# Dense products of a two-layer hybrid decoder step: the 576 tokens as 256 and 320 columns instead of 288 and 288

## The chip, the core and the metric

The kernel runs on one core of one Trainium2 chip. The metric is device time in microseconds for one execution. Column n of a product is token n: the 512 prompt tokens come first, then 8 samples of 8 tokens, 576 in all.

## What is computed

Two decoder layers for a prompt of 512 tokens and 8 samples of 8 tokens each, with shared weights. Cut to what matters here:

```python
h = rmsnorm(x, ln_mix)
parts = split(h @ w_in)                 # 1024 -> 8712 columns: three branches and three gates
o_a = hgrn2(...); o_b = diff_attention(...); o_c = gated_deltanet(...)
mix = sum(sigmoid(gate_i) * (o_i @ w_branch_i))     # 512 -> 1024 each
x = x + mix @ w_out                                 # 1024 -> 1024
g, u = split(rmsnorm(x, ln_ffn) @ w_up)             # 1024 -> 2 * 2816
g = causal_dwconv(g, width 3)
x = x + (silu(g) * u) @ w_down                      # 2816 -> 1024
```

The q, k and v of the gated DeltaNet go through a causal convolution of width 4. All of it is float32, with new states and key and value rows as further outputs.

## The kernel before, in words

Activations lie transposed: features on the 128 partitions, the 576 tokens along the free axis. A dense product takes one 128-column tile of a weight matrix at a time. `dense_steps` (L266) loads it from memory, `split` (L262) makes of it a rounded part `wh` (ScalarE) and the rest `wl` (VectorE), both float32r, four 128x128 blocks at a time; activations are split the same way into `xh` and `xl`. Per block of 128 input features, TensorE then does `xh wh`, `xl wh` and `xh wl`, each in two matmuls because a sum of 576 columns does not fit one PSUM bank: tokens 0 to 287 (`hf` = 0) into one bank and 288 to 575 (`hf` = 1) into another. So a block is six matmuls, each with a weight load of its own, in the order `xh wh`, `xl wh` (first tokens), `xh wh`, `xl wh` (second), `xh wl` (first), `xh wl` (second). The accumulator `acc` is a tile of two banks, of which two alternate (`psA`).

One block's six matmuls go through the helper `mm` (L181, the matmul itself on L189), which also adds `n / 2400` us to a planner's clock `clk`. In the mixing part of a layer `drive` (L317) uses that clock to interleave the products with the recurrences, the attention and their own small float32 matmuls; the order of instructions on every engine is fixed when the program is built. The steps of the run, by the profile's time: start (0 to 20 us), mixing part of layer 0 (20 to 668), the merge of the branches (L1414 on, 668 to 819, with the output projection up to 819 to 825), the convolution MLP (825 to 1233: 22 gate tiles, 22 up tiles, then the down projection in three groups), then the same again for layer 1 to 2449.6.

A finished sum is read out of PSUM by VectorE or ScalarE. Most readers take both halves in one instruction through a view `v2` that cuts the other operand in two; the two convolution inputs need three, since prompt and samples go to different places: `conv_silu` (L721, 24 times, tile `cb`) and the MLP gate (L1476, 44 times, tile `cbf`):

```python
tt(P[:, 2:2 + HALF], acc[:, 0], rb[:, 0:HALF], ALU.mult)                 # 288 columns
tt(P[:, 2 + HALF:514], acc[:, 1, 0:224], rb[:, HALF:SEQ], ALU.mult)      # 224 columns
tt(Ps[:, :, 2:10], acc[:, 1, 224:288]..., rb[:, SEQ:]..., ALU.mult)      # 64 columns
```

Of the kernel before, what the change touches and what calls it, by code (L numbers as in the profile page):

```python
# [10 lines left out]
F32 = mybir.dt.float32  # L11
# [5 lines left out]
ALU = mybir.AluOpType  # L17
# [5 lines left out]
SEQ = 512  # L23
# [4 lines left out]
T = SEQ + NS  # L28
HALF = T // 2
# [117 lines left out]
def kernel(ctx, tc, a, o, depth=DEPTH, dbg=None):  # L147
    nc = tc.nc
    V, S, G, PE = nc.vector, nc.scalar, nc.gpsimd, nc.tensor
# [9 lines left out]
    psA = pool('psA', bufs=2, space=PSUM)  # L159
# [21 lines left out]
    def mm(out, lhsT, rhs, start=True, stop=True, cost=None, **kw):  # L181
        n = math.prod(rhs.shape[1:])
        if lhsT.dtype == F32R:
            clk[0] += n / 2400
        elif lhsT.dtype == BF16:
            clk[0] += 0.107
        else:
            clk[0] += cost or (0.094 if kw else max(n / 600, 0.214))
        PE.matmul(out, lhsT, rhs, start=start, stop=stop, **kw)  # L189
# [5 lines left out]
    def tt(out, in0, in1, op, eng=None):  # L195
        (eng or V).tensor_tensor(out=out, in0=in0, in1=in1, op=op)  # L196
# [27 lines left out]
    for k in range(KD):  # L224
        x_ = px.tile([128, T], F32, name=f'x{k}')
# [40 lines left out]
    def dense_steps(src, xs, M=128, raws=None, nk=None, prime=False):  # L266

        nk, k = nk or len(xs), 0  # L270
        gr = [(k0, min(4, nk - k0)) for k0 in range(0, nk, 4)]
        if raws is None:
            raws = []
            for k0, n in gr:
                raw = wp.tile([128, 512], F32, tag='raw', bufs=4, name='raw')
                nc.sync.dma_start(raw[:, :n * M], src[:, k0 * M:(k0 + n) * M])
                raws.append(raw)

        def weights(g):
            n = gr[g][1] * M  # L280
            wh = wp.tile([128, 512], F32R, tag='wh', bufs=3, name='wh')
            wl = wp.tile([128, 512], F32R, tag='wl', bufs=3, name='wl')
            split(raws[g][:, :n], wh[:, :n], wl[:, :n])
            return wh, wl

        nxt = weights(0)
        if prime:
            yield
        acc = psA.tile([128, 2, 512], F32, tag='acc', name='acc')
        for g, (k0, n) in enumerate(gr):  # L290
            wh, wl = nxt
            for i in range(n):
                if i == min(1, n - 1) and g + 1 < len(gr):
                    nxt = weights(g + 1)
                xh, xl = xs[k]
                cs = slice(i * M, (i + 1) * M)
                for w, xx in ((wh, (xh, xl)), (wl, (xh,))):
                    for hf in range(2):
                        for x_ in xx:
                            mm(acc[:M, hf, :HALF], w[:, cs], x_[:, hf * HALF:(hf + 1) * HALF],  # L300
                               start=(k == 0 and w is wh and x_ is xh), stop=(k == nk - 1 and w is wl))
                k += 1
                if k < nk:
                    yield
        return acc[:, :, :HALF]

    def dense(src, xs):
        return run(dense_steps(src, xs))
# [8 lines left out]
    def drive(stages, fill, xs, pre, psmp):  # L317
# [53 lines left out]
        while True:  # L371
# [41 lines left out]
                assert not live and not stages  # L413
                return
            clk[0] = min(ts)

    def v2(ap):
        return ap.rearrange('p (a b) -> p a b', a=2)

    def norm_in(k, xt, g):  # L420

# [169 lines left out]
    with stage('ln0', 'right') as p0:  # L591
# [12 lines left out]
        rb, rc = norms()  # L604
# [33 lines left out]
    for l in range(depth):  # L638
# [62 lines left out]

        def half(dst, acc):

            V.scalar_tensor_tensor(out=v2(dst), in0=acc, scalar=0.5, in1=v2(rb), op0=ALU.mult, op1=ALU.mult)

        def gate_post(i, acc):
            th = gt.tile([128, T], F32, tag='th', name='thb')
# [13 lines left out]
        def conv_silu(acc, ci, dst):  # L721

            P = cvp.tile([128, 604], F32, tag='cb', name='cb')
            Ps = P[:, 515:603].rearrange('p (b j) -> p b j', j=11)
            G.memset(P[:, 0:3], 0.0)
            G.tensor_copy(Ps[:, :, 0:3], hg[:, ci])
            tt(P[:, 3:3 + HALF], acc[:, 0], rb[:, 0:HALF], ALU.mult)
            tt(P[:, 3 + HALF:515], acc[:, 1, 0:224], rb[:, HALF:SEQ], ALU.mult)
            tt(Ps[:, :, 3:11], acc[:, 1, 224:288].rearrange('p (b j) -> p b j', j=8),
               rb[:, SEQ:].rearrange('p (b j) -> p b j', j=8), ALU.mult)  # L730
            G.tensor_copy(gco[:, ci, 0, :], P[:, 512:515])
            G.tensor_copy(gco[:, ci, 1:9, :], Ps[:, :, 8:11])
            A = cvp.tile([128, 604], F32, tag='ca', name='ca')
            w = F['gconv']
            S.activation(A[:, 0:600], P[:, 0:600], AF.Copy, scale=w[:, 4 * ci:4 * ci + 1])
            for j in range(1, 4):
                V.scalar_tensor_tensor(out=A[:, 0:600], in0=P[:, j:j + 600], scalar=w[:, 4 * ci + j:4 * ci + j + 1],  # L737
                                       in1=A[:, 0:600], op0=ALU.mult, op1=ALU.add)
            th = gt.tile([128, 604], F32, tag='th', name='ct')
            S.activation(th[:, 0:600], A[:, 0:600], AF.Tanh, scale=0.5)  # L740
            sv = lambda t: t[:, 515:603].rearrange('p (b j) -> p b j', j=11)[:, :, 0:8]
            V.scalar_tensor_tensor(out=dst[:, 0:SEQ], in0=th[:, 0:SEQ], scalar=1.0, in1=A[:, 0:SEQ], op0=ALU.add, op1=ALU.mult)
            V.scalar_tensor_tensor(out=dst[:, SEQ:].rearrange('p (b j) -> p b j', j=8), in0=sv(th), scalar=1.0, in1=sv(A),
                                   op0=ALU.add, op1=ALU.mult)
# [246 lines left out]
        def hgrn_head(h, p):  # L991
            f2 = lambda tag, bufs=1: p.tile([128, T], F32, tag=tag, bufs=bufs, name=tag)
            acc = yield win(16 + 4 * h + 0)
            XX, xn = p.tile([128, 2, TP], F32, name='XX'), [0]
# [4 lines left out]
                return XX[:, xn[0] % 2]  # L999

            E = XX[:, 0, 0:T]
            tt(v2(E), acc, v2(rb), ALU.mult)
            S.activation(E, E, AF.Exp, scale=-1.0)
            V.tensor_scalar(out=E, in0=E, scalar1=float(2.0 ** 60), scalar2=None, op0=ALU.min)
            lf, f_, k_, Gc = f2('lf'), f2('f'), f2('k'), f2('G')
# [6 lines left out]
            acc = yield win(16 + 4 * h + 1)  # L1012
            th = gt.tile([128, T], F32, tag='th', name='th')
# [3 lines left out]
            V.scalar_tensor_tensor(out=q_, in0=th, scalar=1.0, in1=hx, op0=ALU.add, op1=ALU.mult)  # L1017
            acc = yield win(16 + 4 * h + 2)
            hv = flip()
            S.copy(v2(hv[:, 0:T]), acc)  # L1020
            vt = p.tile([128, 5, 128], F32, name='vt')
            yield 0.8
            transpose_to(vt, hv, rc)
# [73 lines left out]
            for cc in range(4):  # L1097
                cs = slice(128 * cc, 128 * cc + 128)
# [8 lines left out]
                if cc:  # L1107
                    V.scalar_tensor_tensor(out=Sn, in0=Sc, scalar=eG[:, 128 * cc + 127:128 * cc + 128], in1=pu[:, 0:128],
                                           op0=ALU.mult, op1=ALU.add)
# [30 lines left out]
        def qk_prep(ti, gi, p):  # L1140
            acc = yield win(ti)
            xr = p.tile([128, TP], F32, tag='xr', bufs=2, name='xr')
            G.memset(xr[:, T:], 0.0)
            S.copy(v2(xr[:, 0:T]), acc)
            tm = p.tile([128, 5, 128], F32, tag='tm', bufs=2, name='tm')
            yield 0.9
            transpose_to(tm, xr)
# [33 lines left out]
        def diff_head(h, p):  # L1181
# [3 lines left out]
            acc = yield win(32 + 3 * h + 2)  # L1185
            xr = p.tile([128, TP], F32, tag='xr', bufs=2, name='xr')
            G.memset(xr[:, T:], 0.0)
            S.copy(v2(xr[:, 0:T]), acc)
            vt = p.tile([128, 5, 128], F32, name='vt')
            yield 0.9  # L1190
            transpose_to(vt, xr, rc)
# [218 lines left out]
        p = pmix  # L1410
# [3 lines left out]
        for f in range(KD):  # L1414
            m = p.tile([128, T], F32, tag='m', bufs=2, name='m')
            for i in range(3):
                th = gt.tile([128, T], F32, tag='th', name='th')
                nc.sync.dma_start(th, thd[l][8 * i + f])
                acc = dense(a['w_br'][l, i, f], brs[4 * i:4 * i + 4])
                if i == 0:  # L1420
                    V.scalar_tensor_tensor(out=v2(m), in0=v2(th), scalar=1.0, in1=acc, op0=ALU.add, op1=ALU.mult)
                else:
                    t = p.tile([128, T], F32, tag='ol', bufs=2, name='mt')
                    V.scalar_tensor_tensor(out=v2(t), in0=v2(th), scalar=1.0, in1=acc, op0=ALU.add, op1=ALU.mult)
                    tt(m, m, t, ALU.add)
            xh = pm.tile([128, T], F32R, name=f'mh{f}')
            xl = pm.tile([128, T], F32R, name=f'ml{f}')
            split(m, xh, xl)
            mixs.append((xh, xl))
# [8 lines left out]
        def residual(f, acc, src, dst, keep):  # L1438
            xo = p.tile([128, T], F32, tag='xo', bufs=2, name='xo')
            nc.sync.dma_start(xo, src[f])  # L1440
            xn = keep.tile([128, T], F32, tag=f'x{f}', name=f'x{f}') if keep is not None else p.tile([128, T], F32, tag='xn', bufs=2, name='xn')
            V.scalar_tensor_tensor(out=v2(xn), in0=acc, scalar=0.5, in1=v2(xo), op0=ALU.mult, op1=ALU.add)  # L1442
            nc.sync.dma_start(dst[f], xn)
            return xn

# [16 lines left out]
        for gidx, ng in enumerate(FG):  # L1462
            hid = []
            for i in range(ng):
# [3 lines left out]
                if fi == 0:  # L1468
# [4 lines left out]
                Ps = P[:, 514:594].rearrange('p (b j) -> p b j', j=10)  # L1473
                G.memset(P[:, 0:2], 0.0)
                G.tensor_copy(Ps[:, :, 0:2], hf_[:, fi])
                tt(P[:, 2:2 + HALF], acc[:, 0], rb[:, 0:HALF], ALU.mult)  # L1476
                tt(P[:, 2 + HALF:514], acc[:, 1, 0:224], rb[:, HALF:SEQ], ALU.mult)
                tt(Ps[:, :, 2:10], acc[:, 1, 224:288].rearrange('p (b j) -> p b j', j=8),
                   rb[:, SEQ:].rearrange('p (b j) -> p b j', j=8), ALU.mult)
                G.tensor_copy(fco[:, fi, 0, :], P[:, 512:514])  # L1480
                G.tensor_copy(fco[:, fi, 1:9, :], Ps[:, :, 8:10])
# [12 lines left out]
                                       op0=ALU.add, op1=ALU.mult)  # L1494
                tt(s2, s2, rb, ALU.mult)
                acc = run(g)
                tt(v2(s2), v2(s2), acc, ALU.mult)
                hh = ph.tile([128, T], F32R, tag='hh', bufs=9, name='hh')
                hl = ph.tile([128, T], F32R, tag='hl', bufs=9, name='hl')
                split(s2, hh, hl)  # L1500
# [144 lines left out]
```

## Time and profile before

| | |
|---|---|
| median of 3 runs | 2452.12 us (2451.75 to 2452.2) |
| the profiled execution | 2451.43 us, of which the span from first to last instruction is 2449.6 us |
| TensorE matmuls, weight loads | 2420.2 us busy (99%), 2317.4 us (95%), 19602 each |
| VectorE, ScalarE, GpSimd | 1664.6 us (68%), 1119.8 us (46%), 131.9 us (5%) |
| granted TensorE clock, mean | 0.997 |

PE is the stream of matmuls, PEld that of weight loads, DVE is VectorE, ACT ScalarE, POOL GpSimd, SP the engine that issues most DMAs. A matmul's own duration in the profile holds its way through the array and overlaps its neighbours; what one costs in a stream is the distance from one start to the next, called its pitch below.

### The profile page before, as it was taken

What the parts mean: (1) busy time and instruction counts of PE and PEld (TensorE: products, weight loads), DVE (VectorE), ACT (ScalarE), POOL (GpSimd) and SP (SyncE); (2) the same over time, 40 slices, a digit from 0 to 9 for tenths busy, and PEclk for the clock granted to TensorE, in tenths of its full rate; (3) what the DMA queues carried; (4) which work ended last, traced back from release to release, by engine and by line L of the source; (5) the groups of instructions that cost most, each with busy time, mean ns of one, the idle gap of its engine ahead of it and who ended that gap; (6) DMA issues with size and microseconds to landing.
All of it is one profiled execution on the core that took longest, in us unless ns stands there. A gap on an engine that the chain in (4) does not pass through costs nothing.

```text
span 2449.6 us, 51852 instructions
## 1 busy us (share of the span) xinstructions
PE 2420.2 (99%) x19602; PEld 2317.4 (95%) x19602; DVE 1664.6 (68%) x4156; ACT 1119.8 (46%) x2401; POOL 131.9 (5%) x446
## 2 busy tenths in 40 slices
PE   8999999999999999999999999999999999999999
PEld 7999989899999999999999998988989999999999
DVE  7787787778665663646677877868776556646464
ACT  5556555646433332323455665646554233323232
POOL 1000000100000010101000010100000000001010
PEclk9999999999999999999999999999999999999999
DMA  6234564554465325252442245564635553242524
GB/s 211 94 99 133 163 215 148 181 179 147 132 204 180 118 87 164 83 162 86 145 137 93 92 163 167 181 211 138 220 103 156 181 175 109 91 155 85 165 84 127
DMA packets 222841, 352.90 MB, mean 144 GB/s; under 512 B 36864, under 2 KB 71680, under 8 KB 222592
## 3 DMA queue, kind: packets, MB, share of 16 engines
q1 hardware_dynamic: 221008, 346.78, 44.1%
q8 instruction: 155, 2.54, 0.4%
q10 hardware_dynamic: 1584, 2.82, 0.4%
q14 instruction: 94, 0.77, 0.1%
HBM read 288.90 MB, written 60.60 MB: 143 GB/s over the span
## 4 chain that ended last, share of the span: by engine, by line
PE 89%; DVE 6%; ACT 3%; issue 1%; DMA 1%; SPq 0%; ACTq 0%; DVEq 0%
PE acc L189 72%; PE r L189 13%; PE r L193 3%; DVE dtr L196 1%; DVE wl L196 1%; DMA ctt<-dt 0%; DVE XX L196 0%; DVE s L527 0%; DVE ca L737 0%; ACT wh L263 0%; DMA x<-in_xT 0%; ACT P L1235 0%; ACT ks L773 0%; DMA og<-ogd 0%; DVE ot L196 0%
## 5 line engine op out<-in xcount | busy, mean ns | idle before, releaser
L189 PE MATMUL acc<-xh,wh 128*128 128x288 f32 x3584 | 1019.3, 299 | 4.1 <-ACT wh L263 4.1
L189 PE MATMUL acc<-xl,wh 128*128 128x288 f32 x3584 | 1012.2, 297 | 1.1 <-DVE xl L425 0.9
L189 PE MATMUL acc<-xh,wl 128*128 128x288 f32 x3584 | 767.0, 294 | 5.0 <-DVE wl L196 4.7
L263 ACT CAST wh<-raw 128x512 fp32r<-128x512 f32 x624 | 383.2, 615 | 835.4 <-PE acc L189 787.5
L189 PEld LDWEIGHTS acc<-xh,wh 128*128 128x128 f32 x3584 | 675.1, 188 | 20.1 <-issue 12.7
L189 PEld LDWEIGHTS acc<-xl,wh 128*128 128x128 f32 x3584 | 675.9, 189 | 3.6 <-DVE xl L425 1.8
L189 PEld LDWEIGHTS acc<-xh,wl 128*128 128x128 f32 x3584 | 577.4, 188 | 7.8 <-DVE wl L196 6.8
L196 DVE TENSOR_TENSOR wl<-raw,wh 128x512 fp32r<-128x512 f32 x624 | 423.0, 679 | 178.5 <-ACT wh L263 177.4
L189 PE MATMUL acc<-hl,wh 128*128 128x288 f32 x704 | 196.7, 296 | 0.0
L189 PE MATMUL acc<-hh,wh 128*128 128x288 f32 x704 | 194.3, 292 | 0.0
L189 PE MATMUL acc<-hh,wl 128*128 128x288 f32 x704 | 147.2, 290 | 0.0
L189 PEld LDWEIGHTS acc<-hl,wh 128*128 128x128 f32 x704 | 132.3, 188 | 0.0
L189 PEld LDWEIGHTS acc<-hh,wh 128*128 128x128 f32 x704 | 132.0, 188 | 0.0
L189 PEld LDWEIGHTS acc<-hh,wl 128*128 128x128 f32 x704 | 113.2, 188 | 0.0
L189 PE MATMUL acc<-oL,wh 128*128 128x288 f32 x384 | 108.0, 295 | 0.0
L189 PE MATMUL acc<-oh,wh 128*128 128x288 f32 x384 | 107.3, 295 | 0.0
L196 DVE TENSOR_TENSOR cbf<-acc,rb 128x288 f32<-128x288 f32 x132 | 39.0, 351 | 88.9 <-PE acc L189 85.0
L1486 DVE SCALAR_TENSOR_TENSOR caf<-cbf,fm,caf 128x592 f32<-128x592 f32 x88 | 73.5, 835 | 15.9 <-ACT caf L1484 14.3
L189 PE MATMUL acc<-oh,wl 128*128 128x288 f32 x384 | 81.6, 293 | 0.0
L1442 DVE SCALAR_TENSOR_TENSOR xn<-acc,xo 128x576 f32<-128x576 f32 x40 | 30.3, 758 | 70.8 <-PE acc L189 70.8
L189 PEld LDWEIGHTS acc<-oL,wh 128*128 128x128 f32 x384 | 73.0, 190 | 0.0
L189 PEld LDWEIGHTS acc<-oh,wh 128*128 128x128 f32 x384 | 72.1, 188 | 0.0
(427 smaller groups left out, 3631.1 us busy)
## 6 DMA issues: line engine op xcount, KB each, us to landing
raw<-in_w_in_t SPq DMA_DIRECT2D x272, 256.0 KB
raw<-in_w_up SPq DMA_DIRECT2D x176, 256.0 KB
pg<-in_kT SPq DMA_DIRECT2D x128, 256.0 KB
pg<-in_v SPq DMA_DIRECT2D x128, 256.0 KB
raw<-in_w_dn SPq DMA_DIRECT2D x64, 256.0 KB
xo<-xres SPq DMA_DIRECT2D x56, 288.0 KB
thd<-thb SPq DMA_DIRECT2D x48, 288.0 KB
th<-thd SPq DMA_DIRECT2D x48, 288.0 KB
```

Source lines behind the costliest of these rows:

```text
L189: PE.matmul(out, lhsT, rhs, start=start, stop=stop, **kw)
L193: PE.transpose(out, in_, idm)
L196: (eng or V).tensor_tensor(out=out, in0=in0, in1=in1, op=op)
L263: S.copy(hi, src)
L1442: V.scalar_tensor_tensor(out=v2(xn), in0=acc, scalar=0.5, in1=v2(xo), op0=ALU.mult, op1=ALU.add)
L1486: V.scalar_tensor_tensor(out=A[:, 0:592], in0=P[:, j:j + 592], scalar=w[:, 3 * fi + j:3 * fi + j + 1], in1=A[:, 0:592], op0=ALU.mult, op1= ...
```

## The change

The two halves become 256 and 320 columns. The accumulator is one tile of 1024 columns over two banks; the first 256 tokens go to columns 256 to 511 (the end of the first bank), the other 320 to columns 512 to 831 (the start of the second). So the sums of all 576 tokens lie side by side, and every reader takes a plain 128x576 operand. The three instructions of each convolution input become two, of 512 and 64 columns. Number and order of the matmuls, weight loads and DMAs stay, and `mm` still books (256 + 320) / 2400 us for each pair.

```diff
-        acc = psA.tile([128, 2, 512], F32, tag='acc', name='acc')
+        acc = psA.tile([128, 1024], F32, tag='acc', name='acc')
...
                 for w, xx in ((wh, (xh, xl)), (wl, (xh,))):
-                    for hf in range(2):
+                    for t0, t1 in ((0, 256), (256, T)):
                         for x_ in xx:
-                            mm(acc[:M, hf, :HALF], w[:, cs], x_[:, hf * HALF:(hf + 1) * HALF],
+                            mm(acc[:M, 256 + t0:256 + t1], w[:, cs], x_[:, t0:t1],
                                start=(k == 0 and w is wh and x_ is xh), stop=(k == nk - 1 and w is wl))
...
-        return acc[:, :, :HALF]
+        return acc[:, 256:256 + T]
...
-            V.scalar_tensor_tensor(out=v2(dst), in0=acc, scalar=0.5, in1=v2(rb), op0=ALU.mult, op1=ALU.mult)
+            V.scalar_tensor_tensor(out=dst, in0=acc, scalar=0.5, in1=rb, op0=ALU.mult, op1=ALU.mult)
...
-                tt(P[:, 2:2 + HALF], acc[:, 0], rb[:, 0:HALF], ALU.mult)
-                tt(P[:, 2 + HALF:514], acc[:, 1, 0:224], rb[:, HALF:SEQ], ALU.mult)
-                tt(Ps[:, :, 2:10], acc[:, 1, 224:288].rearrange('p (b j) -> p b j', j=8),
+                tt(P[:, 2:514], acc[:, 0:SEQ], rb[:, 0:SEQ], ALU.mult)
+                tt(Ps[:, :, 2:10], acc[:, SEQ:].rearrange('p (b j) -> p b j', j=8),
                    rb[:, SEQ:].rearrange('p (b j) -> p b j', j=8), ALU.mult)
```

`conv_silu` changes like the last hunk, and the other readers of a sum (the gates, the residual adds, the copies before a transpose, the merge, the product with the up part) like the one above it: `v2(...)` goes, the operands stay.

## Rows read from the trace of the kernel before

**Rows 1.** The page, busy time of each engine: us, share of the span, instructions.
```profile
PE 2420.2 (99%) x19602; PEld 2317.4 (95%) x19602; DVE 1664.6 (68%) x4156; ACT 1119.8 (46%) x2401; POOL 131.9 (5%) x446
```

**Rows 2.** Who PE waited for, the two longest: us in total, times, longest.
```profile
PE acc L189 <- DVE wl L196: 4.7, 6, 2.0
PE acc L189 <- ACT wh L263: 4.1, 2, 2.0
```

**Rows 3.** Groups by line and shape, one matmul of each kind of activation: xcount | busy, mean ns.
```profile
L189 PE MATMUL acc<-xh,wh 128*128 128x288 f32 x3584 | 1019.3, 299 | 4.1 <-ACT wh L263 4.1
L189 PE MATMUL acc<-hh,wh 128*128 128x288 f32 x704 | 194.3, 292 | 0.0
L189 PE MATMUL acc<-oh,wh 128*128 128x288 f32 x384 | 107.3, 295 | 0.0
L189 PE MATMUL acc<-mh,wh 128*128 128x288 f32 x256 | 71.1, 292 | 0.0
```

**Rows 4.** The chain of waits in order of time, unbroken runs of dense matmuls: start, us, count.
```profile
128.64 6.25 PE acc L189 x48
135.44 6.33 PE acc L189 x48
210.52 13.70 PE acc L189 x102
...
666.66 151.64 PE acc L189 x1149
825.18 407.22 PE acc L189 x3132
1877.10 157.60 PE acc L189 x1197
2041.58 404.11 PE acc L189 x3108
```

**Rows 5.** Timeline of PE in the MLP of layer 0: start, us, one matmul.
```profile
900.22 0.29 PE L189 MATMUL acc<-xh,wh 128*128 128x288 f32 x1
900.35 0.30 PE L189 MATMUL acc<-xl,wh 128*128 128x288 f32 x1
```

**Rows 6.** Stretch of layer 0 (columns as in rows 12; clock 0.50), and PE's timeline there.
```profile
398.00:399.50 1.50, 1.50 (x7) 1.50 (x7) 0.76 (x2) 0.00 (x0) 0.00 (x0) 0.50 1.00 361
...
398.81 0.44 PE L189 MATMUL acc<-xl,wh 128*128 128x288 f32 x1
399.05 0.44 PE L189 MATMUL acc<-xh,wh 128*128 128x288 f32 x1
399.29 0.41 PE L189 MATMUL acc<-xl,wh 128*128 128x288 f32 x1
```

**Rows 7.** Timeline, plain float32 matmuls of 256 columns, from two starts, merged: us, count.
```profile
250.42 1.24 PE L189 MATMUL r<-ckq 128*128 128x256 f32 x5
...
250.64 0.81 PE L189 MATMUL r<-ckq 128*128 128x256 f32 x3
```

**Rows 8.** Timeline of PEld in a stream of 64-column float32 matmuls: loads of 128x128.
```profile
611.81 0.97 PEld L189 LDWEIGHTS r<-XX 128*128 128x128 f32 x8
```

**Rows 9.** Timeline, a dense matmul whose successor's weight load comes late: PE, then PEld.
```profile
440.73 0.29 PE L189 MATMUL acc<-xh,wh 128*128 128x288 f32 x1
440.86 0.29 PE L189 MATMUL acc<-xl,wh 128*128 128x288 f32 x1
441.73 0.53 PE L189 MATMUL acc<-xh,wl 128*128 128x288 f32 x2 [0.57 <-DVE wl L196]
...
440.73 0.19 PEld L189 LDWEIGHTS acc<-xl,wh 128*128 128x128 f32 x1
441.73 0.30 PEld L189 LDWEIGHTS acc<-xh,wl 128*128 128x128 f32 x2 [0.80 <-DVE wl L196]
```

**Rows 10.** Timeline of one MLP gate tile's read-out: last matmuls of the sum, then DVE.
```profile
910.75 0.29 PE L189 MATMUL acc<-xh,wl 128*128 128x288 f32 x1
911.14 0.89 DVE L196 TENSOR_TENSOR cbf<-acc,rb 128x288 f32<-128x288 f32 x3 [2.06 <-PE acc L189]
```

**Rows 11.** Groups by line and shape, readers of a sum on DVE.
```profile
L196 DVE TENSOR_TENSOR s<-s,acc 128x576 f32<-128x576 f32 x44 | 33.2, 755 | 11.1 <-PE acc L189 10.7
L196 DVE TENSOR_TENSOR cb<-acc,rb 128x224 f32<-128x224 f32 x24 | 9.1, 380 | 0.0
```

**Rows 12.** Stretches: us, busy us of PE, PEld, DVE, ACT, POOL, then clock, DMA, GB/s.
```profile
20.00:650.00 630.00, 617.62 (x5277) 571.29 (x5275) 483.64 (x1478) 357.08 (x879) 32.88 (x121) 0.99 0.47 150
819.00:1234.00 415.00, 415.00 (x3190) 414.52 (x3190) 242.54 (x414) 141.74 (x220) 30.56 (x91) 1.00 0.37 119
1234.00:1860.00 626.00, 616.33 (x5270) 571.31 (x5268) 478.68 (x1457) 355.66 (x873) 29.89 (x114) 0.99 0.45 146
```

More of the change, by code (lines that the diff above doesn't have):

```diff
@@ L415, in drive @@
             clk[0] = min(ts)
-    def v2(ap):
-        return ap.rearrange('p (a b) -> p a b', a=2)
     def norm_in(k, xt, g):
@@ L726, in conv_silu @@
             G.tensor_copy(Ps[:, :, 0:3], hg[:, ci])
-            tt(P[:, 3:3 + HALF], acc[:, 0], rb[:, 0:HALF], ALU.mult)
-            tt(P[:, 3 + HALF:515], acc[:, 1, 0:224], rb[:, HALF:SEQ], ALU.mult)
-            tt(Ps[:, :, 3:11], acc[:, 1, 224:288].rearrange('p (b j) -> p b j', j=8),
+            tt(P[:, 3:515], acc[:, 0:SEQ], rb[:, 0:SEQ], ALU.mult)
+            tt(Ps[:, :, 3:11], acc[:, SEQ:].rearrange('p (b j) -> p b j', j=8),
                rb[:, SEQ:].rearrange('p (b j) -> p b j', j=8), ALU.mult)
@@ L1001, in hgrn_head @@
             E = XX[:, 0, 0:T]
-            tt(v2(E), acc, v2(rb), ALU.mult)
+            tt(E, acc, rb, ALU.mult)
             S.activation(E, E, AF.Exp, scale=-1.0)
@@ L1019, in hgrn_head @@
             hv = flip()
-            S.copy(v2(hv[:, 0:T]), acc)
+            S.copy(hv[:, 0:T], acc)
             vt = p.tile([128, 5, 128], F32, name='vt')
@@ L1143, in qk_prep @@
             G.memset(xr[:, T:], 0.0)
-            S.copy(v2(xr[:, 0:T]), acc)
+            S.copy(xr[:, 0:T], acc)
             tm = p.tile([128, 5, 128], F32, tag='tm', bufs=2, name='tm')
@@ L1187, in diff_head @@
             G.memset(xr[:, T:], 0.0)
-            S.copy(v2(xr[:, 0:T]), acc)
+            S.copy(xr[:, 0:T], acc)
             vt = p.tile([128, 5, 128], F32, name='vt')
@@ L1420 @@
                 if i == 0:
-                    V.scalar_tensor_tensor(out=v2(m), in0=v2(th), scalar=1.0, in1=acc, op0=ALU.add, op1=ALU.mult)
+                    V.scalar_tensor_tensor(out=m, in0=th, scalar=1.0, in1=acc, op0=ALU.add, op1=ALU.mult)
                 else:
                     t = p.tile([128, T], F32, tag='ol', bufs=2, name='mt')
-                    V.scalar_tensor_tensor(out=v2(t), in0=v2(th), scalar=1.0, in1=acc, op0=ALU.add, op1=ALU.mult)
+                    V.scalar_tensor_tensor(out=t, in0=th, scalar=1.0, in1=acc, op0=ALU.add, op1=ALU.mult)
                     tt(m, m, t, ALU.add)
@@ L1441, in residual @@
             xn = keep.tile([128, T], F32, tag=f'x{f}', name=f'x{f}') if keep is not None else p.tile([128, T], F32, tag='xn', bufs=2, name='xn')
-            V.scalar_tensor_tensor(out=v2(xn), in0=acc, scalar=0.5, in1=v2(xo), op0=ALU.mult, op1=ALU.add)
+            V.scalar_tensor_tensor(out=xn, in0=acc, scalar=0.5, in1=xo, op0=ALU.mult, op1=ALU.add)
             nc.sync.dma_start(dst[f], xn)
@@ L1496 @@
                 acc = run(g)
-                tt(v2(s2), v2(s2), acc, ALU.mult)
+                tt(s2, s2, acc, ALU.mult)
                 hh = ph.tile([128, T], F32R, tag='hh', bufs=9, name='hh')
```

## The prediction, written before the changed kernel was run

> **What bounds the kernel now.** I read the page first: PE is busy 99% of the span and the weight loads 95%, DVE 68% [rows 1]. A busy share alone doesn't say what paces PE, so the second view is who PE waited for: the longest entry is 4.7 us in total, and no read-out of an `acc` is among the longest ones [rows 2]. So PE is fed nearly always, and the question is how long its own stream takes. The groups by line say what the stream is: 3584 + 704 + 384 + 256 = 4928 blocks' `xh wh` matmuls, and as many `xl wh` and `xh wl`, so 3 x 4928 = 14784 dense matmuls of 288 columns, 7392 pairs [rows 3]. The third view, the chain of waits in order of time, gives their pitch, since in a run that nothing breaks the time divided by the count is the pitch: 407.22 / 3132 = 130.0 ns and 404.11 / 3108 = 130.0 ns in the two MLPs, 151.64 / 1149 = 132.0 and 157.60 / 1197 = 131.7 in the merges, and in the mixing parts runs of 130.2, 131.9 and 134.3 (13.70 / 102) [rows 4]. 14784 times about 131 ns is 1937 us of the 2449.6: whatever the change does to the pitch of a pair counts 7392 times, and whatever it does elsewhere counts little.
>
> **What the change leaves alone.** Six matmuls, six weight loads, the same order, the same two banks; the DMAs and their queues don't move, and no wait is put in front of one. The planner books (256 + 320) / 2400 = 0.24 us for a pair, as for 2 x 288, so its clock reads the same at every block's end, and the order on the engines stays. Nothing to add to the sum.
>
> **The pitch of a pair.** This is the one large term, and the trace has no float32r matmul of 256 or 320 columns. At full clock (2.4 GHz) 288 columns are 120.0 ns at a column a cycle; the pitch is 130.0, so 10 ns are over [rows 4, 5]. With the clock at its lower level (1.2 GHz) the pitch is 0.24 us [rows 6], and 288 / 1.2 = 240.0: there nothing is over. What the 10 ns depend on decides:
> - If it is a fixed cost of a matmul, 256 columns take 106.7 + 10 = 116.7 and 320 take 133.3 + 10 = 143.3: 260.0 a pair, as now.
> - If it goes with the columns (a factor 130 / 120), 115.6 + 144.4 = 260.0, as now.
> - If it came from the weight load beside it, 260.0 too, since there are as many loads. But rows speak against that cause: at 440.86 a dense matmul ran with no load beside it, for the next load began only at 441.73, and it lasted 0.29 us, as did its neighbour at 440.73, which had one [rows 9].
>
> All three leave the sum, so the PE term is 0. The bounds from the nearest rows: plain float32 matmuls of 256 columns follow each other every (1.24 - 0.81) / 2 = 215 ns [rows 7]. At two cycles a column that is 213.3, so only about 2 ns over. If the new shapes paid only 2 ns each, a pair would be 240 + 4 = 244: 16 x 7392 = 118 us less. On the other side the dearest run of the same shape has 134.3 [rows 4], 4.3 over the MLPs' pitch: 14784 x (134.3 - 131.0) = 49 us more if all of it went there. I take 0, because the two forms that a cost of this kind can simply have both give it.
>
> **Is a 256-column matmul long enough to hide a weight load?** In a stream of 64-column matmuls loads of the same 128x128 float32 weights follow each other every (0.97 - 0.19) / 7 = 111 ns [rows 8], and there they are the pace, for the columns are far shorter. The 256-column matmul is expected at 115.6 to 116.7: the load fits with some 5 ns to spare, where at 288 it had 19. So no price, but the cover is thin; should the shorter matmul need less than 111, the load takes over as a floor, which limits a gain and adds no loss.
>
> The Trainium skill speaks to this place ("TensorE: Matmul & The Clock Gate", LDWEIGHTS): it gives a load as its columns divided by 1.2 GHz, which is 106.7 ns for 128, exactly the streaming time of 256 columns at 2.4 GHz. That rule speaks against the 256, since it leaves no slack before the extra nanoseconds; the measured 111 ns is 4 above it, and the sum by either stays 0 as long as the excess of the shorter matmul is at least 5 ns.
>
> **The read-outs.** For a convolution input three DVE instructions become two. The three take 0.89 us [rows 10]. They can't become shorter than one reader of all 576 columns, 0.755 [rows 11], so the gain is between 0 and 0.135 us a tile; I take 0.06. On the path it counts only where PE waits for DVE. The 44 MLP tiles lie beside a PE that is busy 415.00 of 415.00 us, with DVE at 242.54 [rows 12]: DVE's slack hides them, they give 0. Of the 24 in the mixing parts, where PE is idle 12 and 10 us in all [rows 12], the most is 24 x 0.135 = 3.2 us; I take 0.5. Nor does joining start the read-out later: the first of the three began at 911.14, after the start of the sum's last matmul, at 910.75, plus its 0.29 [rows 10], so it waited for both halves already. The other readers keep their columns and their instruction count (576 columns in 0.755 us) and lose only a split operand; bounded by their distance from plain ones of the same size, nothing.
>
> **The sum.** The profiled execution takes 2451.43 us, of which 1.83 lie around the span. 2451.43 + 0 (pairs) - 0.5 (read-outs) = 2450.9; the median of the three runs is 0.7 above the profiled one, so 2451.6.
>
> **The rivals.**
> - *The stream settles in another pattern (slower).* The rows show a thing that neither simple form explains: a run has one pitch from end to end, and there are several: 130.0, 131.9, 134.3 [rows 4]. The same six-matmul block thus runs in different stable patterns, and both MLPs, 6240 matmuls, sit in the cheapest. Other lengths make other patterns. If the MLPs settle at 131.9, it is 6240 x 1.9 = 12 us: 2463; at 134.3, 27 us, and with the merges (2346 matmuls, 132 now) 5 more: 2484. The price begins as soon as the MLPs' pitch per matmul passes 130.8, which is 5 us. For it: the present stretches can hardly do better than the best seen. Against: the pattern was the same in both layers, so it isn't drawn by chance, and nothing says that the new one is worse.
> - *Weight loads set the pace (slower, much).* If the 130 ns were the rhythm of load and matmul and not of columns, 256 columns would still take 130 and 320 take 143 to 144: 273.5 a pair, 13.5 x 7392 = 100 us, 2551. It decides if 256-column matmuls start 130 apart. Rows 8 and 9 speak against it: loads go every 111 ns, and the matmul without one lasted as long.
> - *The 10 ns belong to 288 columns (faster).* Then the new shapes pay less, down to the 2 ns of rows 7: 118 us, 2333. In between, 5 ns a matmul would give 250 a pair, 74 us, 2377; from about 9.7 ns down the gain passes 5 us. For it: rows 6 and 7 show streams with nearly no excess. Against: the one case without has the halved clock, the other reads a column every second cycle, so neither asks the array for a float32r column each cycle. The Trainium skill has a rule of this kind (same page, Back-to-back issue gap): a warm matmul takes its columns divided by 2.4 GHz plus 2.5 ns. By it a pair is 245.0, before and after; the 130.0 of this trace stands against 122.5, so the rule misses something that the dense matmuls pay.
> - *The change does nothing at all to the order or the read-outs,* for instance because the joined instruction waits longer than the three did. That is the forecast with 0 in place of 0.5, 2452.1.
>
> **How the numbers follow.** Forecast, pitch of the pair kept within a third of a nanosecond per matmul and a little from the read-outs: 0.38, the last rival included. Another pattern, dearer: 0.32. Weight loads: 0.04. A smaller excess: 0.26, of which about half under 27 us. A measurement of this kernel can tell some 0.2% from no change, 5 us. So faster 0.26, same 0.38, slower 0.36, and the time is 2451.6. The range goes down to 2425, which leaves out about 0.12 of the faster case, and up to 2485, which takes in the pattern of 134.3 in all four long runs and leaves out the weight loads and a little more, 0.06.
>
> **What would show it.** Right: in the chain of waits the two MLP runs are again about 407 and 404 us; in the timeline the starts go 116, 116, 144, 144, 116, 144 ns apart; the loads still last 0.19; two `cbf` instructions in some 0.83. A dearer pattern: the MLP runs at 412 to 420 with the same spacing ratio. Weight loads: the short matmuls 130 apart. A smaller excess: 109 to 112 and 135 to 139, the first against the floor of 111. Wrong altogether would be a PE that waits for an `acc` or for a read-out, or another order of instructions.

## The result, and the profile after

The changed kernel takes 2471.72 us (median of 4 runs, 2470.43 to 2475.1) against 2452.05 for the kernel before, a ratio of 1.009 [1.0078, 1.0103]: 19.7 us slower. The profiled execution took 2475.1 us, its span is 2473.2, 23.6 more than before.

The page, where [rows 1] stood: TensorE is 26.8 us longer busy, VectorE has 68 instructions less (24 + 44 joined read-outs) and 2.7 us less to do.

```profile
PE 2447.0 (99%) x19602; PEld 2344.8 (95%) x19602; DVE 1661.9 (67%) x4088; ACT 1119.3 (45%) x2401; POOL 137.1 (6%) x446
```

Who PE waited for, as in [rows 2]: the same two entries, together 1.1 us more. PE doesn't wait; its own stream takes longer.

```profile
PE acc L189 <- DVE wl L196: 6.1, 6, 2.0
PE acc L189 <- ACT wh L263: 3.8, 2, 1.9
```

The chain of waits in order of time, as in [rows 4] (start, us, count of dense matmuls in an unbroken run):

```profile
58.83 6.40 PE acc L189 x48
...
668.09 152.57 PE acc L189 x1149
827.59 417.65 PE acc L189 x3132
1888.23 159.73 PE acc L189 x1197
2054.90 414.46 PE acc L189 x3108
```

The counts are those of before, so the four long runs can be taken from each other line by line: 417.65 - 407.22 = 10.4, 414.46 - 404.11 = 10.4, 152.57 - 151.64 = 0.9, 159.73 - 157.60 = 2.1. That is 23.8 us, all of the span's 23.6; the mixing parts, dearer products and cheaper read-outs together, came out even. In the MLPs the pitch went from 130.0 ns to 417.65 / 3132 = 133.4.

The timeline of PE in the MLP of layer 0, one block of six and the start of the next (start, us, shape), and the stretch of that MLP (us, busy us of PE, PEld, DVE, ACT, POOL, then granted clock, DMA share, GB/s):

```profile
902.68 0.28 PE L189 MATMUL acc<-xh,wh 128*128 128x256 f32 x1
902.80 0.28 PE L189 MATMUL acc<-xl,wh 128*128 128x256 f32 x1
902.92 0.31 PE L189 MATMUL acc<-xh,wh 128*128 128x320 f32 x1
903.07 0.31 PE L189 MATMUL acc<-xl,wh 128*128 128x320 f32 x1
903.21 0.43 PE L189 MATMUL acc<-xh,wl 128*128 128x256 f32 x2
903.48 0.28 PE L189 MATMUL acc<-xh,wh 128*128 128x256 f32 x1
```
```profile
821.00:1236.00 415.00, 415.00 (x3110) 414.52 (x3111) 233.94 (x380) 135.51 (x213) 32.72 (x89) 1.00 0.36 114
```

A block of six goes from 902.68 to 903.48: 0.80 us. Before, the blocks of this MLP took 407.22 / 522 = 0.780. The granted clock is 1.00 as before, so the 20 ns aren't the clock's. The short matmuls start 0.12 apart, the long ones 0.15: each pays its columns divided by 2.4 GHz (106.7 and 133.3 ns) and some 13 ns more, where the 288 columns paid 10. The read-out of a gate tile is shorter, as foreseen (0.89 before, [rows 10]; DVE now shows two instructions):

```profile
915.75 0.82 DVE L196 TENSOR_TENSOR cbf<-acc,rb 128x512 f32<-128x512 f32 x2 [2.15 <-PE acc L189]
```

### The profile page after: what moved, and what is told of

Same layout as the page of the kernel before. It is cut to its first block, busy times and chain, and to the rows that moved or that the text cites. A ratio compares the mean times of both kernels' runs of the same rounds, so it can differ in the third digit from the quotient of the medians.

```text
span 2473.2 us, 51799 instructions
## 1 busy us (share of the span) xinstructions
PE 2447.0 (99%) x19602; PEld 2344.8 (95%) x19602; DVE 1661.9 (67%) x4088; ACT 1119.3 (45%) x2401; POOL 137.1 (6%) x446
## 4 chain that ended last, share of the span: by engine, by line
PE 91%; DVE 4%; ACT 2%; DMA 2%; issue 1%; SPq 0%; ACTq 0%; DVEq 0%
PE acc L189 74%; PE r L189 13%; PE r L193 3%; DMA ctt<-dt 1%; DVE wl L196 1%; DVE s L524 0%; DMA pg<-in_v 0%; SPq L1277 0%; DMA x<-in_xT 0%; ACT P L1231 0%; ACT ks L769 0%; DMA og<-ogd 0%; ACT wh L263 0%; DVE dtr L196 0%; DMA dt<-dtr 0%
## 5 line engine op out<-in xcount | busy, mean ns | idle before, releaser
L189 PE MATMUL acc<-xl,wh 128*128 128x256 f32 (+1 forms) x3584 | 1044.7, 298 | 1.1 <-DVE xl L422 1.1
L189 PE MATMUL acc<-xh,wh 128*128 128x256 f32 (+1 forms) x3584 | 1006.8, 302 | 3.9 <-ACT wh L263 3.8
L189 PE MATMUL acc<-xh,wl 128*128 128x256 f32 (+1 forms) x3584 | 779.6, 298 | 6.1 <-DVE wl L196 6.1
L189 PE MATMUL acc<-hl,wh 128*128 128x256 f32 x704 | 203.5, 296 | 0.0
L189 PE MATMUL acc<-hh,wh 128*128 128x256 f32 x704 | 193.4, 297 | 0.0
L189 PE MATMUL acc<-hh,wl 128*128 128x256 f32 x704 | 151.2, 297 | 0.0
L189 PE MATMUL acc<-oL,wh 128*128 128x256 f32 (+1 forms) x384 | 110.3, 296 | 0.0
L189 PE MATMUL acc<-oh,wh 128*128 128x256 f32 (+1 forms) x384 | 105.0, 295 | 0.0
L189 PE MATMUL acc<-oh,wl 128*128 128x256 f32 (+1 forms) x384 | 82.0, 294 | 0.0
L189 PE MATMUL acc<-ml,wh 128*128 128x256 f32 (+1 forms) x256 | 74.0, 296 | 0.0
```

## The experiments

**The lengths alone, and which comes first.** The first kernel keeps everything of the change, the sums side by side and the joined read-outs, but takes 288 and 288 again (the sums then lie at columns 224 to 799). The second has the long part first, (0, 320) and (320, T), from column 192 on.

```diff
-                    for t0, t1 in ((0, 256), (256, T)):
+                    for t0, t1 in ((0, 288), (288, T)):
...
-                            mm(acc[:M, 256 + t0:256 + t1], w[:, cs], x_[:, t0:t1],
+                            mm(acc[:M, 224 + t0:224 + t1], w[:, cs], x_[:, t0:t1],
```

> The changed kernel with its lengths undone alone: 288 and 288 columns, but the sums still side by side across the two banks (columns 224 to 511 and 512 to 799) and the read-outs still joined. Theory 1, the lengths 256 and 320 stream dearer per column (the changed kernel's blocks of six take 800.0 ns, the ones before 780.0): the MLP blocks go back to 780 ns, 130.0 a matmul, and the whole to 2450 to 2452 us. Rival, the place in PSUM or the joined read-outs cost it: it stays at about 2471 us, 133.3 a matmul.

> The changed kernel with the long piece first: 320 and 256 columns (PSUM columns 192 to 511 and 512 to 767). Theory 1 (each length has its own cost, 118.4 ns for 256 and 148.3 for 320): again 800 ns a block and 2471 us. Rival, the order of short and long among the six matmuls makes the pattern: another time of a block, 780 to 810 ns, and the whole 2445 to 2490 us.

Measured: 2445.14 us, ratio 0.9981 [0.9969, 0.9993], and 2472.85, ratio 1.0085 [1.0068, 1.0102]. The MLP runs of the first, then of the second, in the chain of waits:

```profile
820.95 407.22 PE acc L189 x3132
2032.58 404.11 PE acc L189 x3108
```
```profile
824.76 417.65 PE acc L189 x3132
2050.87 414.46 PE acc L189 x3108
```

To the last digit these are the runs of the kernel before and of the changed kernel. So, with the tiles where they lie, the lengths cost all of it, 2471.7 - 2445.1 = 26.6 us; a sum that crosses from one bank to the next costs nothing, nor does the order of short and long count. And the rest of the change is a small gain, which the next pair prices.

**The read-outs alone.** Both kernels have 288 and 288 and the sums side by side; the one reads a convolution input in three instructions again, the other (the first kernel above once more) in two.

```diff
-            tt(P[:, 3:515], acc[:, 0:SEQ], rb[:, 0:SEQ], ALU.mult)
+            tt(P[:, 3:3 + HALF], acc[:, 0:HALF], rb[:, 0:HALF], ALU.mult)
+            tt(P[:, 3 + HALF:515], acc[:, HALF:SEQ], rb[:, HALF:SEQ], ALU.mult)
```

> The 288 and 288 side by side of the first run, with the read-outs of the convolution inputs cut in three again (288, 224, 64 columns). Theory: the joined read-outs are what the first run has over the kernel before; then this one falls back to the kernel before, some 6 us behind the joined one (2451 against 2445 us). Rival: they are hidden, as the prediction had it (0.5 us, at most 3.2), and the first run's gain has another source; then the two agree within 3 us.

> The first run's kernel once more, as the partner of the one with three read-outs: MLP blocks of six at 780 ns, the whole at 2445 us, 0.2% under the kernel before.

Measured: 2450.3 us, ratio 0.9997 [0.9987, 1.0007], and 2445.39, ratio 0.9977 [0.9966, 0.9988]; the two ran on the same chip. Sums side by side, with plain operands for every reader, are alone worth nothing that shows; the joined instructions bring 4.9 us, by the ratios 0.2%. The MLP runs, three reads first:

```profile
825.35 407.22 PE acc L189 x3132
2041.38 404.11 PE acc L189 x3108
```
```profile
823.48 407.22 PE acc L189 x3132
2035.47 404.11 PE acc L189 x3108
```

Their lengths are alike; the joined one starts the first 1.9 us earlier and the second 5.9 us earlier, which is the whole difference of the spans (2449.4 and 2443.5). So the gain arises ahead of the MLPs, and the 44 gate tiles in them give nothing. The same kernel's two profiles differ by some 3 us at these places (820.95 and 823.48, 2032.58 and 2035.47), so the size stays 5 us give or take 3.

About half of it is granted clock. The same steps of layer 1 in the two profiles, three reads first (the stretch, columns as in [rows 12], and a matmul of PE within it):

```profile
1826.00:1838.00 12.00, 10.50 (x63) 10.26 (x61) 5.18 (x18) 2.90 (x5) 0.00 (x0) 0.72 0.37 118
...
1828.34 0.43 PE L189 MATMUL r<-TB,ap 128*128 128x64 f32 x2 [1.50 <-DVE TB L196]
```
```profile
1823.00:1835.00 12.00, 11.41 (x96) 11.18 (x95) 7.56 (x24) 4.76 (x8) 0.00 (x0) 1.00 0.52 163
...
1825.82 0.43 PE L189 MATMUL r<-TB,ap 128*128 128x64 f32 x2 [0.59 <-DVE TB L196]
```

With three reads PE stood idle for 1.50 us there, waiting for VectorE's tile `TB` (0.59 with two), and then ran at the lower of its two clock levels; the lead of the joined kernel grows from 2.5 us at these matmuls to 5.9 at the next MLP. Over all their runs the mean granted clock is 0.997 against 0.998, and 0.001 of such a span is 2.4 us. The runs of either kernel that were granted 0.998 have medians of 2447.4 and 2445.5 us, 1.9 apart. By what way the read-outs would bring about that wait no run shows.

**The pitch of each length by itself.** The changed kernel runs in full, and behind it 24 bursts of 16 blocks of six float32r matmuls, on one token tile and one weight tile, with other lengths and other places in PSUM; their sums go to a scratch tile that nothing uses.

> The changed kernel, and behind its end 24 bursts of 16 blocks of the same six matmuls each, on one token tile and one weight tile, that no other engine works beside: pairs of lengths 288+288, 256+320, 272+304, 264+312, 280+296, their reverse, and the same with equal lengths from 256 to 512. Theory 1: in the bursts too 288+288 takes 780 to 790 ns a block and 256+320 takes 800, wherever the sums lie; the other lengths say whether the excess is a fixed one (some 10 ns at every length), goes with the columns (8 to 11% at every length), or has steps. Rival, the cost comes from the other engines' work or from PSUM places: all pairs of 576 take the same in the bursts, or the bursts differ by the place of the sums.

The timeline of the bursts; of each burst the first matmul of two blocks, ten blocks apart (288 and 288; 256 and 320; all six 256; all six 320; all six 512):

```profile
2797.88 0.29 PE L1570 MATMUL pacc<-ph,qh 128*128 128x288 f32 x1
2805.68 0.29 PE L1570 MATMUL pacc<-ph,qh 128*128 128x288 f32 x1
...
2810.40 0.28 PE L1570 MATMUL pacc<-ph,qh 128*128 128x256 f32 x1
2818.40 0.28 PE L1570 MATMUL pacc<-ph,qh 128*128 128x256 f32 x1
...
2588.68 0.28 PE L1570 MATMUL pacc<-ph,qh 128*128 128x256 f32 x1
2595.88 0.28 PE L1570 MATMUL pacc<-ph,qh 128*128 128x256 f32 x1
...
2650.00 0.31 PE L1570 MATMUL pacc<-ph,qh 128*128 128x320 f32 x1
2658.80 0.31 PE L1570 MATMUL pacc<-ph,qh 128*128 128x320 f32 x1
...
2755.52 0.39 PE L1570 MATMUL pacc<-ph,qh 128*128 128x512 f32 x1
2769.12 0.39 PE L1570 MATMUL pacc<-ph,qh 128*128 128x512 f32 x1
```

Ten blocks of 288 and 288 take 7.80 us and of 256 and 320 take 8.00: the bursts repeat the 780 and the 800 ns of the MLPs with no other work beside them, so no cast, read-out or transfer has a part in it. The uniform bursts give the form of the cost: 256 columns 7.20 / 60 = 120.0 ns, 320 columns 146.7, 512 columns 226.7, each 13.3 over its columns divided by 2.4 GHz, and so did 352 and 384. That is a cost per matmul, not per column; but it isn't one constant, for 416, 448 and 480 columns paid 15.5, 16.0 and 17.8 in the same program. The other lengths by the same reading: 272 + 304, 280 + 296 and 264 + 312 all about 793 ns a block; 288 + 288 in a second burst of the same program 790; 256 + 320 took 800 wherever in PSUM its sums lay and in either order.

**A split between the two.** The changed kernel with 272 and 304.

```diff
-                    for t0, t1 in ((0, 256), (256, T)):
+                    for t0, t1 in ((0, 272), (272, T)):
```

> 272 and 304 columns, sums side by side, read-outs joined. In the bursts of the probe a block of these lengths took 793 ns against 800 for 256 and 320 and 780 to 790 for 288 and 288. Theory (the lengths alone set it, and bursts and kernel agree): MLP runs at 793 / 6 = 132.2 ns a matmul, 414 and 411 us, and the whole some 2464 blocks times 7 ns = 17 us under the changed kernel, 2455 us. Rival (the kernel's stretches settle elsewhere than the bursts): MLP runs at another pitch, 130 or 133.3.

Measured: 2458.82 us, ratio 1.003 [1.0019, 1.0042], with this MLP run:

```profile
822.59 414.17 PE acc L189 x3132
```

414.17 / 522 = 793.4 ns a block, what the burst had said: here the burst carries over to the kernel. The whole kernel came out 12.9 us under the changed one, not the 17 expected; the two MLPs have some 7 of them.

**What the 10 to 13 ns come from.** 23 bursts behind the changed kernel, as above, each with one thing changed: the order of the six, one matmul repeated, weights of 64 columns in place of 128, no accumulation (each matmul starts its sum anew), lengths a few columns off 288, and bfloat16 tokens and weights.

> Bursts behind the changed kernel again, 23 of them, to find what the fixed cost of a dense matmul hangs on: other orders within the block of six, one matmul repeated on one bank, weights of 64 columns in place of 128 (half the weight load), no accumulation, lengths close to 288, other starts in the token tile, bfloat16 in place of float32r. If the weight load causes the cost, 64 columns of weights bring 256+320 from 800 to some 735 ns a block; if the float32r read causes it, bfloat16 alone does (288+288 at 735 or less) and 64-column weights stay at 780 to 800; if accumulation or the change of bank does, the bursts without one or the other drop.

The timeline: 256 and 320 with weights of 64 columns, two blocks ten apart; then 191 bfloat16 matmuls in one run, first 288 and 288, then 256 and 320 (the row names the first shape).

```profile
2599.93 0.28 PE L1580 MATMUL pacc<-ph,qh 128*64 128x256 f32 x1
2607.73 0.28 PE L1580 MATMUL pacc<-ph,qh 128*64 128x256 f32 x1
...
2709.82 23.56 PE L1580 MATMUL pacc<-xb,wb 128*128 128x288 bf16 x191
```

With bfloat16 the pitch is (23.56 - 0.29) / 190 = 122.5 ns on average over both splits: 2.5 over the columns, and 735 ns a block for either. With half the weight columns, 256 and 320 falls from 800 to 780, less than a third of the way to 735, and 288 and 288 from 790 to 784. Without accumulation nothing changes (790 and 800), nor with one matmul of 256, 288 or 320 columns repeated on one token tile, one weight tile and one bank (720, 790 and 880 for six). Two other orders of the six took 288 and 288 from 790 to 800. 284 + 292 and 276 + 300 took 800, and 280 + 296 had taken 793: the cost doesn't rise steadily away from 288. The excess, then, comes with float32r, and in part with the number of weight columns. Whether it is the arithmetic of float32r or the reading of 4-byte elements these bursts don't tell; if the second, it lies in the two reads that feed TensorE, of tokens and of weights.

**Where the reads start.** 42 bursts of 10 blocks behind the changed kernel, with the tokens, the weights or both starting some elements further on in their tiles.

> Bursts of 10 blocks behind the changed kernel once more, 288+288 and 256+320, now with the token columns or the weight columns starting 2 to 128 elements further into their tiles. In the last probe 256-column float32r matmuls starting 8 elements in took 700 ns a block against 720 at 0, so where the reads start has a share in the fixed cost. Theory (reads of tokens and of weights get in each other's way, by where they start): 256+320 falls from 800 to 780 ns or under at some offsets of either, 288+288 moves as well. Rival (the cost hangs on the lengths alone): every offset gives 800 for 256+320 and 780 to 790 for 288+288.

The timeline, two blocks seven apart in each burst: 256 and 320 with both at 0; 256 and 320 with the weights at 16; 288 and 288 with the weights at 16; 288 and 288 with the weights at 64; 288 and 288 with the tokens at 2.

```profile
2570.33 0.28 PE L1549 MATMUL pacc<-ph,qh 128*128 128x256 f32 x1
2575.93 0.28 PE L1549 MATMUL pacc<-ph,qh 128*128 128x256 f32 x1
...
2721.32 0.28 PE L1549 MATMUL pacc<-ph,qh 128*128 128x256 f32 x1
2726.83 0.28 PE L1549 MATMUL pacc<-ph,qh 128*128 128x256 f32 x1
...
2681.68 0.29 PE L1549 MATMUL pacc<-ph,qh 128*128 128x288 f32 x1
2687.28 0.29 PE L1549 MATMUL pacc<-ph,qh 128*128 128x288 f32 x1
...
2697.62 0.29 PE L1549 MATMUL pacc<-ph,qh 128*128 128x288 f32 x1
2703.08 0.29 PE L1549 MATMUL pacc<-ph,qh 128*128 128x288 f32 x1
...
2482.71 0.30 PE L1549 MATMUL pacc<-ph,qh 128*128 128x288 f32 x1
2488.35 0.30 PE L1549 MATMUL pacc<-ph,qh 128*128 128x288 f32 x1
```

Divided by seven these are 800, 787, 800, 780 and 806 ns a block. Over all starts 288 and 288 takes anything from 780 to 807, and 256 and 320 from 787 to 807: with the weights 16 elements on, 256 and 320 is the cheaper one. Over the 21 pairs of starts the two splits average the same, 795 and 794 ns. With tokens and weights both 8 elements on, each split is back at its value for both at 0 (790 and 800), and with tokens 8 and weights 16 on it has the value for 0 and 8 (793 for either), so the start of the one against the other counts. It isn't all that counts: with tokens 8 and weights 4 on, or 4 and 8, the blocks (791 and 787, 792 and 797) don't match those with the same distance from 0 (800 and 793, 807 and 794). In these bursts, then, the two splits have no price of their own; they have one together with where the reads start.

**The same in the kernel.** If that is so, the changed kernel must become faster when its weight tiles are moved by 64 bytes against the token tiles. Gap tiles that nothing uses do it (the two together move all that lies behind the weights by 128 elements); the second kernel is the one with 288 and 288 and joined read-outs, moved by 64 elements (gap tiles of 64 and 64).

```diff
     cst = pool('cst', bufs=1)
+    gap0 = pool('gap0', bufs=1)
     wp = pool('wp', bufs=2)
+    gap1 = pool('gap1', bufs=1)
     xp = pool('xp', bufs=8)
...
+    gap = gap0.tile([128, 16], F32, name='gap0'), gap1.tile([128, 112], F32, name='gap1')
```

> The changed kernel (256 and 320 tokens) with one thing altered: the weight tiles lie 16 elements (64 bytes) further on against the token tiles, by a small unused gap tile on either side of them. In the bursts a block of six at 256/320 took 800 ns with both reads starting alike, and 789 (784 to 793) with the weights 16 elements on. Theory (the fixed part of a dense matmul is set by where the reads of tokens and weights stand to each other): the long runs on TensorE fall from 800 ns a block to 784 to 793, 417.65 us to about 409 to 414 in the larger MLP run, and the kernel's time from 2471.7 to 2440 to 2460 us. Rival (the lengths 256 and 320 alone set it, and the bursts were a peculiarity of one token tile read again and again): blocks stay at 800, 417.65 us, and the time at 2471. Second rival (in the kernel tokens and weights come from many tiles with many relative starts, so that a shift only exchanges one pattern for another): a mixture of 790 to 807, and 2460 to 2480.

> The kernel with 288 and 288 tokens, sums side by side and joint read-outs, with the weight tiles 64 elements (256 bytes) further on against the token tiles. In the bursts a block of six at 288/288 took 790 ns with both reads starting alike and 780 with the weights 64 elements on. Theory (relative start sets the fixed part): the mixing parts and merges, now at 790 to 807 ns a block, come to 780 as well; some 1000 blocks at 10 to 27 ns each would be 10 to 20 us, so about 2425 to 2435 us against 2445. Rival (the lengths set it, or many relative starts are mixed in the kernel anyway): no block shorter on the whole, 2440 to 2455.

Measured: 2453.93 us, ratio 1.0017 [1.0008, 1.0027], and 2447.8, ratio 0.9986 [0.9976, 0.9996]. The MLP runs of the moved 256 and 320:

```profile
824.65 411.86 PE acc L191 x3132
2041.01 408.72 PE acc L191 x3108
```

411.86 / 522 = 789.0 ns a block; the burst had 787. 64 bytes took back 17.8 of the 26.6 us, with the lengths, the order and the read-outs as in the changed kernel. The 288 and 288 gained nothing from its 64 elements: its MLP runs stay at 407.22 and 404.11, and the expected 10 to 20 us in the mixing parts and merges didn't come. A token tile is 576 columns, 64 more than four times 128, so its tiles probably stand 0 and 64 off in turn and a shift of 64 only exchanges them; that is argued, not shown.

**Two controls.** In the first the tokens and all that lies behind them move by 128 elements, as above, and the weights don't (there is no `gap0`); in the second the weights move by 32.

```diff
+    G.memset(gap1.tile([128, 128], F32, name='gap1'), 0.0)
...
+    gap = gap0.tile([128, 32], F32, name='gap0'), gap1.tile([128, 96], F32, name='gap1')
```

> A control for the shift of 16 elements, which had brought the changed kernel from 2471.7 to 2453.9 us. There the pools behind the weights (tokens and the rest) had moved by 128 elements (512 bytes) as well, by the two gap tiles together. Here they move by the same 128 and the weights stay where they were: one gap tile of 128 elements behind the weights. Theory (the step of 16 elements between weights and tokens counts, and a whole 128 changes nothing in it): blocks back at 800 ns, the larger MLP run at 417.65 us, 2465 to 2475 us. Rival (anything that moves the tokens' place breaks the pattern of 800; a burst with the tokens 128 elements on took 793): about 793 a block, 414 us, 2453 to 2462 us.

> The changed kernel with the weights 32 elements (128 bytes) on, the pools behind them 128 as before. The burst at 256/320 took 797 ns a block with the weights 32 on, against 789 with 16 and 800 with none. Theory (the bursts give the size of each shift): about 797 a block, the larger MLP run at about 416 us, some 6 us under the changed kernel, 2460 to 2470 us. Rival (any shift that isn't a whole 128 does the same): 789, 412 us, 2454 us.

Measured: 2469.76 us, ratio 1.0076 [1.0053, 1.0099], and 2467.61, ratio 1.0063 [1.0038, 1.0087]. The larger MLP run of the first, then of the second:

```profile
824.21 417.65 PE acc L190 x3132
```
```profile
826.33 416.50 PE acc L191 x3132
```

The first is back at the changed kernel's 417.65, so it was the 16 elements between weights and tokens that helped, not the move as such. The second has 416.50 / 522 = 797.9 ns a block, against 797 in the burst. One reading of the bursts didn't carry over: tokens 128 elements on took 793 there, and the kernel with that shift stayed at 800.

## Why the prediction was wrong

The forecast was no change, 2451.6 us; it became 2471.7, inside the range, by the rival that was given 0.32.

- *The pitch of a pair.* This is the step that failed: "I take 0, because the two forms that a cost of this kind can simply have both give it." Of the two, the runs bear out the fixed cost per matmul (120.0, 146.7 and 226.7 ns for 256, 320 and 512 columns). But the sum over a pair is kept only if the fixed cost has the same size at each length, and in the MLPs it was 10.0 at 288 and on average 13.3 at 256 and 320. The term is not 0 but 20 ns a block in the MLPs, 0.020 x 1040 blocks = 20.8 us there and 3.0 in the merges.
- *The rows that said so were in hand.* The runs of before show 130.0, 131.9 and 134.3 ns for one and the same shape [rows 4]. A cost that has several values for one shape isn't a constant of the matmul, and the MLPs sat on the lowest of them. The prediction used this for a rival and for its upper bound, and still made the forecast from a constant. Had it priced the change by the spread of these rows, it would have leaned to slower: over the 21 starts of the bursts either split averages 794 to 795 ns a block, and the MLPs of before had 780. One reading of these rows goes too far: the merges' 132.0 and 131.7 are means of blocks that, in the trace of before, mostly took 780 to 794 ns, so a run need not have one pitch from end to end.
- *The first rival* had mechanism, place and size: MLP runs at 412 to 420 us (417.65 and 414.46 came), starts in the same spacing, PE waiting for nothing new. By its own working, (133.35 - 130.0) x 6240 = 20.9 us on the forecast gives 2472.5. What it called a pattern hangs, by the bursts and the shifted kernels, on where the weights' reads start against the tokens'; that the new pattern would be a dearer one the prediction could argue only from the MLPs sitting on the best value seen.
- *Is a 256-column matmul long enough?* As predicted: no price. The short matmuls start some 118 ns apart in the changed kernel, above the 111 of [rows 8], and not 130, so the weight loads don't set the pace and the rival of 2551 us falls. Yet the loads aren't without a part: weights of half the width took 20 ns off a block of 256 and 320 and 6 off one of 288 and 288. [rows 9] couldn't have shown it: they compare the durations of two matmuls, 0.29 us each at a pitch of 0.13, and a load's price would stand in the pitch.
- *The rival that the 10 ns belong to 288 columns* is the wrong way round: 288 was the cheaper. The rule that it named is in the Trainium skill ("TensorE: Matmul & The Clock Gate", Back-to-back issue gap): columns divided by 2.4 GHz plus 2.5 ns. It is met exactly by the bfloat16 burst, 122.5 ns for 288 columns, and by no float32r run here.
- *The read-outs.* The direction and the size of one tile were right (0.07 us less, 0.06 taken), and the 44 in the MLPs gave nothing, as said. The term was put too low: 0.5 us, at most 3.2, against 4.9 measured. 24 tiles of 0.07 us are 1.7 us, about what runs of the same granted clock differ by (1.9); the rest goes with the granted clock, 0.997 against 0.998. The sum had no term for what a wait of PE does to its clock.
- *What the change leaves alone* held: the same counts in the runs of the chain, and PE's waits within 1.1 us.

The two parts of the change thus work against each other: the lengths cost 26.6 us and the joined read-outs, with the sums side by side, give 5 to 7 back. The kernel with 288 and 288 and joined read-outs keeps the second without the first: 2445.1 to 2445.4 us, ratios 0.9981 and 0.9977, some 0.2% under the kernel before.

## What to carry to other kernels

If one instruction shape shows several pitches in one trace, its overhead depends on something besides the shape; a new shape must then be priced by that whole spread, and mostly upward where the present stretch sits on its lowest value. A dozen blocks of the new shape in a burst behind the kernel gave its pitch here within 10 ns in 800, mostly within 2; one burst shows one start of the reads, though, and the kernel may have others. And a change of several parts is worth taking apart even when it loses, since the winning part can stay.

## What the runs showed of the hardware

- A float32r matmul with its own 128x128 weight load paid 10 to 14.4 ns over its columns at 2.4 GHz for lengths of 240 to 384 and 512, and 15.5 to 17.8 for 416 to 480; bfloat16 paid 2.5 in blocks of 288 and 288 and of 256 and 320.
- That excess hung on where in SBUF the weights' reads start against the tokens': 780 to 807 ns for the same six matmuls, and 64 bytes of shift were worth 17.8 us (0.7%) of this kernel. Whether the matmuls accumulate changed nothing; another place in PSUM changed nothing that a second program repeated; another order of the six changed a block of 288 and 288 by up to 10 ns. Why the starts matter inside the chip no run here shows.
- One VectorE instruction reads 512 columns across the border of two PSUM banks without a price that shows: two instructions took 0.82 us where three took 0.89.
